# Three moves in the order of a hybrid pooling and attention block: products with the softmax reciprocals, sums of the h blocks, and one staging buffer

## The chip, the cores and the metric

The kernel runs on one core of one Trainium2 chip. The metric is the device time of one execution in microseconds (us). The kernel before takes 721.88 us, the median of three runs (721.56 to 722.66). Engines are named as the profile names them: PE (matmul), DVE (vector), ACT (scalar), POOL (GpSimd) and SP, whose queue issues most of the transfers.

## The reference

One decoder block on 1024 tokens, with 16 learned meta tokens ahead of them, all in float32:

```python
h = rmsnorm(concat(meta, x), norm_g)                                   # (1040, 1024)
u, z_pool, q, k, v, z_attn, f, g_pool, g_attn = split(h @ w_in)
y_pool = causal_multiscale_pool(u, pool_w, pool_scale) * silu(z_pool)  # windows 2, 4, 8, 16
y_attn = forgetting_attention(q, k, v, log_sigmoid(f + b_forget)) * silu(z_attn)   # 8 heads of 64
merged = sigmoid(g_pool) * (y_pool @ w_up_pool) + sigmoid(g_attn) * (y_attn @ w_up_attn)
out = rmsnorm(x + merged @ w_out, final_norm_g)
```

The attention is a causal softmax whose logits carry a running sum of the forget gates. The kernel leaves its rows unnormalised at first, sums the exponentials on the way, and multiplies the result y by the reciprocals of these sums later.

## The kernel before

Every float32 matrix is split into a high part and a remainder, and a product is made of three matmuls (high with high, high with remainder, remainder with high). The high part is copied by ACT, the remainder is a subtraction on POOL or DVE. Each weight tile thus goes through SP (load `raw`), ACT (`whi`), POOL (`wlo`), and then PE can use it.

The work has five stages, with their place in the profiled execution:

- **Projection steps (0 to 62 us, L495 to L574).** x is normalised, transposed on PE and split into `hh` and `hl` (L261). Between the transposes the first head pair is projected in twelve steps n = 0 to 11 (L526): q, k and v for four stretches of tokens. Each step of n > 3 also forms one half of a block of h, the sum or negated sum of `hh` and `hl` in a tile `f` of 128 x 1024 on DVE (`h_block`, L170), and stores it to DRAM (L177), where later sums build on it. SP's other transfers of these steps are small parameters (L553 to L555), the early weights of the next head pair (`load_raw`, L482), the pooling weights `pw` (L567) and copies from DRAM to DRAM that wait in a list and are issued one per step, and five more at the end (`copies`, L179, `gs` and `td`).
- **Attention (62 to 425 us).** 16 units of one head and 512 queries each. PE's gaps in them are filled from a list of projections (`Fill`, L415): first q of pair 1 (whose weights were loaded early), then u of group 3 (`f_u`, L403), then k of pair 1, and so on. `w_chunk` (L199) loads the weights of such a projection and splits them.
- **Chunks (425 to 551 us, L1147 to L1298).** z_pool, z_attn and half of g_attn are formed with seven block products n = 0 to 6 in place of eight, each in six chunks i of 12 matmuls with 512 columns (`g_prod`, L1059). A chunk is named (n, i). The loop at L1235 goes through them: it splits the weights of the chunk four places on (`w_split`, L1020), issues the matmuls of the chunk two places on, moves the result of the chunk before out of its PSUM bank (`evict`, L1104), and then does what the table `extra` (L1199) has for this chunk. Chunks with i > 3, and those of n = 1, 3 and 4, share four banks in rotation (`gb_`, L1054), so chunk (4, 5) writes the bank that (4, 1) wrote four chunks before and cannot start until `evict` has read that one.
- **Up projections (551 to 638 us)** and **output product and norm (638 us to the end).**

The table `extra` holds among others: `rc_in` (L926), which loads the reciprocals, one per head and query, from DRAM into `rc`; `attn_norm` (L932), one DVE multiplication of a 128 x 1024 tile y by `rc`; `pool_split` (L963), which splits a pooled group into `plh` (ACT) and `pll` (DVE); and `h_split` (L1037), which splits two halves of a block of h into `gh`, which the chunks of the next n multiply with. In n = 5 the order of i is 3, 2, 1, 0, 4, 5.

What sets the order: PE's order is that of the code everywhere (L88). In the projection steps and in the chunks the order of all engines is that of the code (L461 to L579, L1165 to L1300). Elsewhere a scheduler of the framework orders ACT, DVE, POOL and SP, and it may put an instruction of the attention stage among those of the projection steps. Each engine, and SP's queue, works strictly in its order: an instruction that waits holds up all behind it. SP's transfers use eight completion semaphores in turn, so SP issues a transfer only when the eighth before it has landed.

The pool `ap_` has six buffers with the tag "s" for the tiles of x, of `f`, for `pw` and later for the scores `S`; the pool `stg` has two with the tag "st" for results on their way to DRAM.

Of the kernel before, what the change touches and what calls it, by code (L numbers as in the profile page):

```python
# [8 lines left out]
F32 = mybir.dt.float32  # L9
# [44 lines left out]
def tile_hybrid_block(ctx, tc, x, meta, norm_g, w_in, b_forget, pool_w, pool_scale,  # L54
# [115 lines left out]
    def h_block(blk, k):  # L170
        f = ap_.tile([128, 2, 512], F32, name="f", tag="s", bufs=6)
        hi, lo = [hblock(d, blk)[:, k:k + 2] for d in (hh4, hl4)]
        if blk in ("12", "21"):
            nc.vector.scalar_tensor_tensor(f, hi, -1.0, lo, op0=ALU.mult, op1=ALU.subtract)
        else:
            nc.vector.tensor_tensor(f, hi, lo, op=ALU.add)
        nc.sync.dma_start(rows_of(HS[{"12": "C", "21": "X"}.get(blk, blk)])[:, k:k + 2], f)  # L177
# [345 lines left out]
    todo, early = [], {}  # L523
    for t0, t1 in ((0, 256), (256, 512), (512, 768), (768, L)):
        todo += [("q", t0, min(t1, SEQ)), ("k", t0, t1), ("v", t0, t1)]
    for n, (kind, t0, t1) in enumerate(todo):  # L526
        if n + 4 < 8:
            xts[n + 4] = norm_load(n + 4)
        if kind == "q":
            run(q_piece(0, wq, t0, t1))  # L530
        elif kind == "k":
            run(k_piece(0, wk, t0, t1))
        else:
            g = v_piece(0, wv, t0, t1)
            run(g)
        i = {0: 2, 1: 3, 3: 4, 4: 5, 5: 8, 6: 6, 7: 7}.get(n)
        if i is not None:
            norm_t(i, xts[i], ntok(i))
        if n == 0:
            hv_ = split_hi(rv, gp, "g")  # L540
            wv = split_lo(rv, hv_, gp, "g")
            VT[0] = gp.tile([128, L], F32, name="vt", tag="g")
            v_alloc(0)
        if n > 3:
            h_block(("11", "12", "22", "21")[n // 2 - 2], n % 2 * 2)
        i = {1: 4, 2: 5, 3: 8, 4: 6, 5: 7}.get(n)
        if i is not None:
            norm_scale(xts[i], ntok(i), norm_stat(xts[i], ntok(i)))
        if n == 2:
            zero_q(0)  # L550
        if n == 4:
            wf = at_.tile([128, KO, H], F32, name="wf", bufs=1)
            nc.sync.dma_start(wf, w_in2[:, :, COL_F:COL_F + H])  # L553
            nc.sync.dma_start(bfb, bass.AP(tensor=b_forget.tensor, offset=b_forget.offset, ap=[[0, 128], [1, H]]))
            nc.sync.dma_start(psc, pool_scale[0].rearrange("(g c) -> c g", c=128))  # L555
        if n == 8:
            wfs = at_.tile([128, KO, 2 * H], F32R, name="wfs", bufs=1)
            nc.vector.tensor_copy(wfs[:, :, :H], wf)
            nc.vector.tensor_tensor(wfs[:, :, H:], wf, r32(wfs[:, :, :H]), op=ALU.subtract)
        if n == 4:  # L560
            early["q"] = load_raw(COL_Q + 128)
        if n == 6:
            early["k"] = load_raw(COL_K + 128)
        if n > 3:
            copies(1)
        if n == 7:
            pw = ap_.tile([128, 4, 128], F32, name="pw", tag="s", bufs=6)  # L567
            nc.sync.dma_start(pw, pool_w[0].rearrange("g c d -> c g d"))
        if n == 10:
            nc.scalar.activation(pwh, pw, AF.Copy)  # L570
            nc.gpsimd.tensor_tensor(pwl, pw, r32(pwh), op=ALU.subtract)
        if n in (4, 7, 10):
            run(v_blocks(0, *range(max(1, 2 * (n // 3) - 2), 2 * (n // 3))))
# [358 lines left out]
    def attn_norm(p):  # L932
        nc.vector.tensor_tensor(Y[p], Y[p], RC[p], op=ALU.mult)
# [103 lines left out]
    def h_split(n):  # L1037
        op_h[n] = [[hq.tile([128, 2, 512], F32R, name="gh", tag="h") for _ in range(2)] for _ in range(2)]
        hi, lo = op_h[n]
        for k in range(2):  # L1040
            nc.scalar.activation(hi[k], raw_h[n][k], AF.Copy, scale=-1.0 if n == 2 else 1.0)
        for k in range(2):
            if n == 2:
                nc.vector.scalar_tensor_tensor(lo[k], raw_h[n][k], -1.0, r32(hi[k]), op0=ALU.mult, op1=ALU.subtract)
            else:
                nc.vector.tensor_tensor(lo[k], raw_h[n][k], r32(hi[k]), op=ALU.subtract)
# [30 lines left out]
    def silu(z, ps, scale=1.0):  # L1077
        evacs.append(nc.scalar.activation(z, ps, AF.Silu, scale=scale))  # L1078
# [112 lines left out]
    def steps_of(g):  # L1191
# [26 lines left out]
        (3, 4): [lambda: h_in(6)],  # L1218
        (3, 5): [lambda: pool_split(2)],
        
        (4, 1): [lambda: attn_norm(0), lambda: h_split(5)],
        (4, 2): [lambda: attn_norm(1), lambda: rc_in(2)],
        (4, 3): [lambda: pool_split(1)],
        (4, 4): [lambda: rc_in(3)],
        (5, 3): [lambda: h_split(6)],
        (5, 2): [lambda: attn_norm(2)],
        (5, 1): [lambda: attn_norm(3)],
        (5, 0): [lambda: pool_split(0), lambda: silu(za[0][:, T0_], za[0][:, T0_])],
        (5, 4): [lambda: silu(za[1][:, T0_], za[1][:, T0_]), lambda: silu(za[2][:, T0_], za[2][:, T0_])],
        (6, 4): [lambda: silu(za[3][:, T0_], za[3][:, T0_])],  # L1230
    }
    AH = 4
# [276 lines left out]
```

## Time and profile before

| what | value |
|---|---|
| median of three runs | 721.88 us |
| the profiled execution: its own time, its span | 722.76 us, 721.0 us |
| PE busy | 707.9 us, 98% of the span |
| DVE, ACT, POOL busy | 72%, 58%, 47% |
| DMA | 129.89 MB, mean 180 GB/s |

The span is the time from the first to the last instruction of the profiled execution; its own time has some 1.8 us more around it. In the rows of the timeline the columns are the start in us, the length in us, the engine, the line of the code, the operation with the tile it writes and those it reads, the shape, and how often it was repeated; in brackets stands how long the engine was idle before and what ended that. SPq rows are issues of transfers, not their landing. Rows of the waits name who waited, for whom, for how long in total, how often, and the longest.

### The profile page before, as it was taken

How to read it: one execution, taken by the hardware profiler on the slowest of the kernel's cores; microseconds unless marked ns; L12 is line 12 of the kernel's file. 1: busy time of each engine (PE TensorE's matmuls, PEld its weight loads, DVE VectorE, ACT ScalarE, POOL GpSimd, SP SyncE). 2: the span in 40 equal slices, each digit the busy share in tenths (PEclk: the TensorE clock that was granted, in tenths of full speed). 3: DMA queues.
4: the chain of work that ended last, by engine and by line, in shares of the span. 5: the costliest groups of instructions: out<-in, count | busy, mean ns of one | idle time of the engine just before them, and what ended most of it. 6: DMA issues, size and time to landing. Idle time of an engine off the chain costs nothing.

```text
span 721.0 us, 10896 instructions
## 1 busy us (share of the span) xinstructions
PE 707.9 (98%) x3613; PEld 610.3 (85%) x3613; DVE 517.5 (72%) x917; ACT 419.8 (58%) x928; POOL 340.6 (47%) x463
## 2 busy tenths in 40 slices
PE   8999999999999999999999999999899999999996
PEld 6997999998899888998888888888688888888885
DVE  5784488476888777787776937984867645888775
ACT  7654477676767779676666522445556332535445
POOL 5423247476275847566296832354882010007152
PEclk9999999999999999999999999999999999999998
DMA  9099987956534485556648459689808366761006
GB/s 315 21 303 359 334 255 173 216 121 161 118 106 100 126 210 128 142 112 132 171 144 214 110 182 348 187 214 284 254 31 273 117 220 236 267 229 59 0 1 233
DMA packets 95354, 129.89 MB, mean 180 GB/s; under 512 B 11457, under 2 KB 62657, under 8 KB 93266
## 3 DMA queue, kind: packets, MB, share of 16 engines
q1 hardware_dynamic: 91776, 110.32, 48.1%
q0 software_dynamic: 2224, 16.25, 12.2%
q10 hardware_dynamic: 1298, 2.63, 1.0%
q8 instruction: 28, 0.46, 0.2%
q14 instruction: 28, 0.23, 0.1%
HBM read 102.25 MB, written 58.39 MB: 223 GB/s over the span
## 4 chain that ended last, share of the span: by engine, by line
PE 93%; DVE 3%; ACT 2%; issue 1%; POOL 0%; POOLq 0%; ACTq 0%; DVEq 0%
PE pj L217 53%; PE pj L1070 12%; PE pj L1389 8%; PE po L794 5%; PE pt L1070 4%; PE pt L1389 2%; PE ps L730 2%; PE ps L729 2%; PE pj L590 1%; DVE pl L776 1%; PE pt L279 1%; PE pj L730 1%; PE pj L729 1%; ACT qa L315 1%; PE pn L279 0%
## 5 line engine op out<-in xcount | busy, mean ns | idle before, releaser
L217 PE MATMUL pj<-hh,whi 128*128 128x512 f32 (+3 forms) x576 | 127.1, 347 | 0.2 <-DVE ka L337 0.2
L217 PE MATMUL pj<-hh,wlo 128*128 128x512 f32 (+3 forms) x576 | 127.2, 346 | 0.0
L217 PE MATMUL pj<-hl,whi 128*128 128x512 f32 (+3 forms) x576 | 126.8, 345 | 0.0
L217 PEld LDWEIGHTS pj<-hh,whi 128*128 128x128 f32 x576 | 97.2, 188 | 10.7 <-PE pj L217 0.5
L217 PEld LDWEIGHTS pj<-hh,wlo 128*128 128x128 f32 x576 | 96.8, 188 | 10.0
L217 PEld LDWEIGHTS pj<-hl,whi 128*128 128x128 f32 x576 | 96.5, 188 | 9.7
L208 POOL TENSOR_TENSOR wlo<-raw,whi 128x256 fp32r<-128x256 f32 x100 | 74.8, 780 | 61.3 <-PE pj L217 31.7
L784 POOL TENSOR_TENSOR acc<-acc,S 128x256 f32<-128x256 f32 (+2 forms) x128 | 90.7, 728 | 8.3 <-ACT S L771 4.1
L776 DVE TENSOR_TENSOR pl<-S,ph 128x512 fp32r<-128x512 f32 (+4 forms) x112 | 80.0, 736 | 15.5 <-ACT ph L775 14.9
L1032 POOL TENSOR_TENSOR gw<-graw,gw 128x256 fp32r<-128x256 f32 x52 | 46.7, 928 | 52.8 <-ACT gw L1025 52.6
L1070 PE MATMUL pj<-gh,gw 128*128 128x512 f32 x276 | 66.2, 397 | 3.4 <-ACT zp L1078 3.4
L1070 PEld LDWEIGHTS pj<-gh,gw 128*128 128x128 f32 x276 | 52.6, 191 | 15.1 <-ACT zp L1078 3.8
L743 DVE TENSOR_TENSOR pt<-pt,S 128x400 f32<-128x400 f32 (+2 forms) x96 | 46.6, 485 | 20.7 <-ACT S L734 18.4
L771 ACT ACTIVATE S<-S 128x512 f32<-128x512 f32 (+4 forms) x112 | 50.3, 481 | 12.8 <-DVE S L770 12.5
L775 ACT ACTIVATE ph<-S 128x512 fp32r<-128x512 f32 (+4 forms) x112 | 52.7, 483 | 3.1 <-PE po L794 2.2
L770 DVE TENSOR_TENSOR S<-S,pt 128x512 f32<-128x512 f32 (+4 forms) x112 | 50.0, 499 | 0.6
L1025 ACT ACTIVATE gw<-graw 128x512 fp32r<-128x512 f32 x38 | 23.2, 623 | 36.6 <-DMA graw<-gs 18.9
L1282 DVE TENSOR_TENSOR rl<-pj,rl 128x512 f32<-128x512 f32 x32 | 22.0, 690 | 28.5 <-PE pj L217 27.8
L784 POOL TENSOR_TENSOR acc<-S 128x256 f32<-128x256 f32 (+1 forms) x32 | 29.6, 950 | 23.6 <-ACT S L771 20.5
L734 ACT ACTIVATE S<-ps,negc 128x16 f32<-128x16 f32 (+4 forms) x65 | 33.1, 514 | 10.4 <-PE ps L730 9.7
L794 PE MATMUL po<-ph,V 128*128 128x512 f32 (+4 forms) x112 | 36.4, 325 | 0.0
L1389 PE MATMUL pj<-opw 128*128 128x512 f32 (+1 forms) x168 | 36.2, 374 | 0.0
(249 smaller groups left out, 1392.7 us busy)
## 6 DMA issues: line engine op xcount, KB each, us to landing
raw<-in_w_in_dram SPq DMA_DIRECT2D x27, 512.0 KB, 6.4
gs<-in_w_in_dram SPq DMA_DIRECT2D x15, 512.0 KB, 9.9
gs<-gs POOLq DMA_DIRECT2D x4, 1536.0 KB, 13.2
graw<-gs SPq DMA_DIRECT2D x12, 512.0 KB, 7.9
td<-in_w_out_dram SPq DMA_DIRECT2D x10, 512.0 KB, 11.5
graw<-in_w_in_dram SPq DMA_DIRECT2D x9, 512.0 KB, 5.7
xt<-in_x_dram SPq DMA_DIRECT2D x8, 512.0 KB, 6.5
accd<-acc SPq DMA_DIRECT2D x16, 256.0 KB, 2.6
```

Of the source, the lines that this page charges most:

```text
L208: ins = nc.gpsimd.tensor_tensor(lo[:, k:k + 2], raw[:, k:k + 2], r32(hi[:, k:k + 2]), op=ALU.subtract)
L217: nc.tensor.matmul(ps, a, b, start=(i == 0), stop=(i == len(seq) - 1))
L743: nc.vector.tensor_tensor(m[:kb, c0:], m[:kb, c0:], s[:kb, c0:], op=ALU.max)
L770: nc.vector.tensor_tensor(s[:kb, c0:], s[:kb, c0:], self.pm[:kb, c0:], op=ALU.subtract)
L771: exps.append(nc.scalar.activation(s[:kb, c0:], s[:kb, c0:], AF.Exp))
L775: nc.scalar.activation(ph[:kb, c0:], s[:kb, c0:], AF.Copy)
L776: dves.append(nc.vector.tensor_tensor(pl[:kb, c0:], s[:kb, c0:], r32(ph[:kb, c0:]), op=ALU.subtract))
L784: accs.append(nc.gpsimd.tensor_tensor(acc[:kb, c:c1], (S0 if b == 1 else acc)[:kb, c:c1], s[:kb, c:c1], op=ALU.add))
L794: nc.tensor.matmul(self.po[:, c0:], v, self.P[b][i][:kb, c0:], start=(b == 0 and i == 0), stop=(b == self.nb - 1 and i == 1))
L1032: nc.gpsimd.tensor_tensor(op[:, 1, k:k + 2], raw[:, k:k + 2], r32(op[:, 0, k:k + 2]), op=ALU.subtract)
L1070: nc.tensor.matmul(ps, stat(n, i, p, k), op_h[n][q][k // 2][:, k % 2], start=fresh and m == 0, stop=m == 11, skip_group_check=True)
L1389: nc.tensor.matmul(ps, pick(A_, k, p)[:, i * 128:(i + 1) * 128], pick(B_, k, q)[:, c0:c1], start=start and n == 0, stop=n == 11, skip_grou ...
```

## The change

Three edits, and no computation is added or taken away. The eight halves of the h blocks are formed in steps 6 to 11 in place of one per step from 4 to 11: two each in steps 8 and 11. The tile `pw` comes from the pool `stg` in place of `ap_`. In the chunks `attn_norm(0)` moves from (4, 1) to (4, 3), `attn_norm(1)` from (4, 2) to (4, 4), `pool_split(1)` from (4, 3) to (4, 5) with `rc_in(3)` behind it, `attn_norm(3)` from (5, 1) to (5, 4) and `pool_split(0)` from (5, 0) to (5, 5).

```diff
--- before.py
+++ after.py
@@ -523,6 +523,8 @@
     todo, early = [], {}
     for t0, t1 in ((0, 256), (256, 512), (512, 768), (768, L)):
         todo += [("q", t0, min(t1, SEQ)), ("k", t0, t1), ("v", t0, t1)]
+    blocks = {6: [("11", 0)], 7: [("11", 2)], 8: [("12", 0), ("12", 2)], 9: [("22", 0)], 10: [("22", 2)],
+              11: [("21", 0), ("21", 2)]}
     for n, (kind, t0, t1) in enumerate(todo):
         if n + 4 < 8:
             xts[n + 4] = norm_load(n + 4)
@@ -541,8 +543,8 @@
             wv = split_lo(rv, hv_, gp, "g")
             VT[0] = gp.tile([128, L], F32, name="vt", tag="g")
             v_alloc(0)
-        if n > 3:
-            h_block(("11", "12", "22", "21")[n // 2 - 2], n % 2 * 2)
+        for blk, k in blocks.get(n, ()):
+            h_block(blk, k)
         i = {1: 4, 2: 5, 3: 8, 4: 6, 5: 7}.get(n)
         if i is not None:
             norm_scale(xts[i], ntok(i), norm_stat(xts[i], ntok(i)))
@@ -564,7 +566,7 @@
         if n > 3:
             copies(1)
         if n == 7:
-            pw = ap_.tile([128, 4, 128], F32, name="pw", tag="s", bufs=6)
+            pw = stg.tile([128, 4, 128], F32, name="pw", tag="st")
             nc.sync.dma_start(pw, pool_w[0].rearrange("g c d -> c g d"))
         if n == 10:
             nc.scalar.activation(pwh, pw, AF.Copy)
@@ -1218,15 +1220,17 @@
         (3, 4): [lambda: h_in(6)],
         (3, 5): [lambda: pool_split(2)],
         
-        (4, 1): [lambda: attn_norm(0), lambda: h_split(5)],
-        (4, 2): [lambda: attn_norm(1), lambda: rc_in(2)],
-        (4, 3): [lambda: pool_split(1)],
-        (4, 4): [lambda: rc_in(3)],
+        (4, 1): [lambda: h_split(5)],
+        (4, 2): [lambda: rc_in(2)],
+        (4, 3): [lambda: attn_norm(0)],
+        (4, 4): [lambda: attn_norm(1)],
+        (4, 5): [lambda: pool_split(1), lambda: rc_in(3)],
         (5, 3): [lambda: h_split(6)],
         (5, 2): [lambda: attn_norm(2)],
-        (5, 1): [lambda: attn_norm(3)],
-        (5, 0): [lambda: pool_split(0), lambda: silu(za[0][:, T0_], za[0][:, T0_])],
-        (5, 4): [lambda: silu(za[1][:, T0_], za[1][:, T0_]), lambda: silu(za[2][:, T0_], za[2][:, T0_])],
+        (5, 0): [lambda: silu(za[0][:, T0_], za[0][:, T0_])],
+        (5, 4): [lambda: attn_norm(3), lambda: silu(za[1][:, T0_], za[1][:, T0_]),
+                 lambda: silu(za[2][:, T0_], za[2][:, T0_])],
+        (5, 5): [lambda: pool_split(0)],
         (6, 4): [lambda: silu(za[3][:, T0_], za[3][:, T0_])],
     }
     AH = 4
```

In the order of instructions on the engines this shows as follows. First SP in the projection steps, from the last load of x (`xt_394`) on; `f` are the halves of the h blocks, `wf`, `bfb` and `psc` small parameters, the first `raw` the early weights of q of pair 1, `gs5` a copy from DRAM to DRAM. Before:

```order
L248 DMA xt_394<-in_x_dram 128x1024
L177 DMA hs11_137<-f_491 128x2x512
L553 DMA wf_501<-in_w_in_dram 128x8x8
L554 DMA bfb_122<-in_b_forget_dram 128x8
L555 DMA psc_121<-in_pool_scale_dram 128x4x1
L482 DMA raw_505<-in_w_in_dram 128x8x128
L181 DMA gs5_136<-in_w_in_dram 256x512
L177 DMA hs11_137<-f_553 128x2x512
```

And now:

```order
L248 DMA xt_394<-in_x_dram 128x1024
L555 DMA wf_498<-in_w_in_dram 128x8x8
L556 DMA bfb_122<-in_b_forget_dram 128x8
L557 DMA psc_121<-in_pool_scale_dram 128x4x1
L482 DMA raw_502<-in_w_in_dram 128x8x128
L181 DMA gs5_136<-in_w_in_dram 256x512 x2
L177 DMA hs11_137<-f_603 128x2x512
```

Six transfers that stood behind the first or the second store of an h block now stand ahead of the first.

Second, SP at the end of these steps. `raw_1013` holds the weights of u of group 3, the second projection that PE takes in the attention stage. Before, the scheduler had it right behind `pw`:

```order
L181 DMA gs1_132<-in_w_in_dram 256x512
L568 DMA pw_662<-in_pool_w_dram 128x4x128
L202 DMA raw_1013<-in_w_in_dram 128x8x128
L177 DMA hs22_138<-f_697 128x2x512
L181 DMA gs1_132<-in_w_in_dram 256x512
```

Now it stands behind the last two of the copies, `td5` and `td1`, that end these steps:

```order
L177 DMA hsX_142<-f_812 128x2x512
L181 DMA gs3_134<-in_w_in_dram 256x512
L181 DMA gs3_134<-in_w_in_dram 512x256
L181 DMA td5_131<-in_w_out_dram 256x512 x2
L181 DMA td1_127<-in_w_out_dram 256x512 x2
L202 DMA raw_1013<-in_w_in_dram 128x8x128
L181 DMA gs2_133<-in_w_in_dram 256x512 x2
```

The load of `raw_1013` moved from the 28th place of SP's transfers to the 41st; the transfers up to the 41st place are the same set in both. On ACT and POOL the split of these weights (`whi_1019`, `wlo_1020`) moved later with it; on PE nothing changed its place.

Third, DVE in the chunks of n = 4, from the eviction of (4, 0) on (`zp_5217`); `zp_5219`, `zp_5221` and `zp_5223` are the evictions of (4, 1), (4, 2) and (4, 3), `gh` the split of the block of h for n = 5, `y` with `rc` is `attn_norm`. Before:

```order
L1081 TENSOR_TENSOR zp_5217<-pj_5212,zp_5217 128x512
L933 TENSOR_TENSOR y_5441<-y_5441,rc_5775 128x1024
L1046 TENSOR_TENSOR gh_5865<-hraw_5643,gh_5863 128x1024
L1046 TENSOR_TENSOR gh_5866<-hraw_5644,gh_5864 128x1024
L1029 TENSOR_TENSOR gw_5871<-graw_5708,gw_5871 128x512
L1081 TENSOR_TENSOR zp_5219<-pj_5213,zp_5219 128x512
L933 TENSOR_TENSOR y_5535<-y_5535,rc_5778 128x1024
L1081 TENSOR_TENSOR zp_5221<-pj_5214,zp_5221 128x512
L967 TENSOR_TENSOR pll_5915<-u_5292,plh_5914 128x1024
L1081 TENSOR_TENSOR zp_5223<-pt_5215,zp_5223 128x512
```

And now:

```order
L1083 TENSOR_TENSOR zp_5217<-pj_5212,zp_5217 128x512
L1048 TENSOR_TENSOR gh_5864<-hraw_5643,gh_5862 128x1024
L1048 TENSOR_TENSOR gh_5865<-hraw_5644,gh_5863 128x1024
L1031 TENSOR_TENSOR gw_5870<-graw_5708,gw_5870 128x512
L1083 TENSOR_TENSOR zp_5219<-pj_5213,zp_5219 128x512
L1083 TENSOR_TENSOR zp_5221<-pj_5214,zp_5221 128x512
L935 TENSOR_TENSOR y_5441<-y_5441,rc_5775 128x1024
L1083 TENSOR_TENSOR zp_5223<-pt_5215,zp_5223 128x512
L935 TENSOR_TENSOR y_5535<-y_5535,rc_5778 128x1024
```

The first multiplication with the reciprocals stands behind the split of the h block, one weight split and the evictions of (4, 1) and (4, 2), all of which stood behind it before.

## The prediction

> **What bounds the kernel now.** I read the page first: the span, the busy times, then the row of PE in 40 slices.
>
> ```profile
> span 721.0 us, 10896 instructions
> PE 707.9 (98%) x3613; PEld 610.3 (85%) x3613; DVE 517.5 (72%) x917; ACT 419.8 (58%) x928; POOL 340.6 (47%) x463
> PE   8999999999999999999999999999899999999996
> ```
>
> PE is busy for 98%. Only 13.1 us are left in which a change of order can bring matmuls closer together, and any wait that it makes on PE is added to the time in full. So I asked next for PE's waits, which name almost all that is not start and end:
>
> ```profile
> PE pj L1070 <- ACT zp L1078: 3.4, 1, 3.4
> PE pt L279 <- DVE hl L282: 0.8, 1, 0.8
> PE pt L279 <- DVE hl L271: 0.2, 1, 0.2
> ```
>
> One wait of 3.4 us lies in the chunks, two small ones in the projection steps. These are the places that the change touches. The timeline of the chunks shows where the long one comes from (rows of several engines in order of time):
>
> ```profile
> 495.60 0.68 DVE L1081 TENSOR_TENSOR zp<-pj,zp 128x512 f32<-128x512 f32 x1
> 498.42 2.00 ACT L1041 ACTIVATE gh<-hraw 128x1024 fp32r<-128x1024 f32 x2
> 498.45 2.37 SPq L930 DMA_DIRECT2D rc<-recs  x4
> 501.77 2.88 PE L1070 MATMUL pj<-gh,gw 128*128 128x512 f32 x12
> 503.18 1.23 DVE L933 TENSOR_TENSOR y<-y,rc 128x1024 f32<-128x1024 f32 x1 [6.89 <-DMA rc<-recs]
> 504.32 2.35 DVE L1046 TENSOR_TENSOR gh<-hraw,gh 128x1024 fp32r<-128x1024 f32 x2
> 506.60 0.68 DVE L1029 TENSOR_TENSOR gw<-graw,gw 128x512 fp32r<-128x512 f32 x1
> 507.20 0.69 DVE L1081 TENSOR_TENSOR zp<-pj,zp 128x512 f32<-128x512 f32 x1
> 508.03 4.57 PE L1070 MATMUL pj<-gh,gw 128*128 128x512 f32 x12 [3.38 <-ACT zp L1078]
> ```
>
> DVE stands 6.89 us at the first `attn_norm`, whose reciprocals are on their way from DRAM. Behind it on DVE stand the split of the h block, a weight split and the eviction of (4, 1), which ends at 507.89. PE starts (4, 5) at 508.03: that chunk writes the bank of (4, 1). The row of the waits names an ACT instruction that ended just then (507.96), but it is the eviction that PE needed. The wait costs more than its length, as the windows show (us, PE busy with its instructions, the clock granted, DMA share, GB/s):
>
> ```profile
> 500.00:504.40 4.40, 4.40 (x21) 1.00 1.00 236
> 504.60:508.00 3.40, 0.05 (x1) 1.00 1.02 364
> 509.00:512.30 3.30, 3.30 (x9) 0.50 1.08 263
> ```
>
> After the pause the clock is at half for 3.3 us, so (4, 5) takes 4.57 us.
>
> **The change part by part: the chunks.** A chunk takes 2.72 us (2.88 less the overlap of 0.16 with the next). Without the wait (4, 5) would follow at 501.77 + 2.72 = 504.5 and its successor at 507.2. That one began at 508.03 + 4.57 less 0.16, 512.4. At stake are 5.2 us: 3.5 of pause and 1.7 of half clock.
>
> In the new order DVE goes from `zp` (to 496.3) to the split of the h block as soon as ACT has its halves (about 499.5 and 500.4), to 501.9; the weight split to 502.5; the eviction of (4, 1) to 503.2, 1.3 us before PE wants the bank. The eviction of (4, 2) ends at 503.8, and only then comes the first `attn_norm`, 0.6 us after the time at which it ran before (503.18). The second follows at about 505.5. What is late next? The pooling split now stands at (4, 5), its ACT half behind two Silu instructions and its DVE half ending about 509.7. The weights of (5, 2), (5, 1) and (5, 4) are finished on POOL, in turn with sums that wait for the evictions:
>
> ```profile
> 500.39 1.44 POOL L136 TENSOR_TENSOR zp<-zp 128x256 f32<-128x256 f32 x2
> 507.96 3.38 POOL L136 TENSOR_TENSOR zp<-zp 128x256 f32<-128x256 f32 x2 [6.13 <-DMA hraw<-hs]
> 515.04 1.90 POOL L1032 TENSOR_TENSOR gw<-graw,gw 128x256 fp32r<-128x256 f32 x2
> ```
>
> From the eviction at 503.2 on, with the slow price of the sum (3.38, once it took 1.44): sum to 506.6, weights of (5, 2) to 508.5, sum to 511.9, weights of (5, 1) to 513.8. PE would start (5, 1) at 512.6 and reach the remainder after eight matmuls, at 514.4. So 0.6 us are left at the least. `rc_in(3)` comes behind the split whose tile it overwrites, at about 510 to 513, lands by 520, and `attn_norm(3)` asks for it at about 519; behind that stand only a weight split and evictions that PE needs after 523. `pool_split(0)` feeds the last of the four pooling products. I cost these moves at nothing; a failing cover costs one to three us. Chunks: **-5.2 us**, between -5.3 and -3.
>
> **The projection steps.** DVE and PE around the first two halves of the h blocks:
>
> ```profile
> 33.43 1.22 DVE L176 TENSOR_TENSOR f<-hh,hl 128x1024 f32<-128x1024 f32 x1
> 36.79 1.22 DVE L176 TENSOR_TENSOR f<-hh,hl 128x1024 f32<-128x1024 f32 x1
> 37.02 0.63 PE L279 MATMUL pt<-ident,xt 128*128 128x128 f32 x4 [0.15 <-DVE hl L271]
> 38.77 0.75 DVE L258 SCALAR_TENSOR_TENSOR xt<-xt,rstd,gb 128x512 f32<-128x512 f32 x1 [0.77 <-POOL rstd L126]
> 40.98 1.29 DVE L282 TENSOR_TENSOR hl<-pt,hh 128x512 fp32r<-128x512 f32 x2
> 41.73 0.65 PE L279 MATMUL pt<-ident,xt 128*128 128x128 f32 x4 [0.77 <-DVE hl L282]
> ```
>
> Without the first `f` all of DVE up to the last scaling of x comes 1.1 us earlier, and both waits of PE go, with some 0.2 us of starting up behind them: PE is 0.15 + 0.77 + 0.2 = **1.1 us** ahead from 42 us on. The moved halves lie where DVE waited anyway; the doubled ones of step 11 end near 57, before DVE is needed for the gates.
>
> The stores and loads matter more. These are SP's issues around the place, and the landings of single transfers, the last number of the rows from the DMA view (of the first store at 34.67, the raw load at 51.34 and the copy at 63.43):
>
> ```profile
> 15.81 0.33 SPq L248 DMA_DIRECT2D xt<-in_x_dram  x1
> 34.67 0.38 SPq L177 DMA_DIRECT2D hs<-f  x1
> 51.34 0.37 SPq L202 DMA_DIRECT2D raw<-in_w_in_dram  x1
> 63.43 1.63 SPq L181 DMA_DIRECT2D td<-in_w_out_dram  x1
> ```
>
> ```profile
> hs<-f SPq DMA_DIRECT2D x1, 512.0 KB, 2.9
> raw<-in_w_in_dram SPq DMA_DIRECT2D x1, 512.0 KB, 5.7
> td<-in_w_out_dram SPq DMA_DIRECT2D x1, 512.0 KB, 14.9
> ```
>
> ```profile
> 20.00:34.00 14.00, 14.00 (x123) 13.84 (x122) 10.56 (x18) 10.32 (x25) 6.38 (x13) 1.00 0.01 2
> 42.00:80.00 38.00, 38.00 (x246) 32.59 (x245) 21.43 (x48) 16.22 (x37) 12.28 (x15) 1.00 1.05 352
> ```
>
> From 42 to 80 us the DMA engines are saturated (share 1.05), and what is queued lands ever later after its issue. Before, the weights of u of group 3 were loaded at 51.34 and landed at 57.0. Their split and use:
>
> ```profile
> 57.05 1.15 ACT L206 ACTIVATE whi<-raw 128x512 fp32r<-128x512 f32 x2 [0.57 <-DMA raw<-in_w_in_dram]
> 57.76 3.40 POOL L208 TENSOR_TENSOR wlo<-raw,whi 128x256 fp32r<-128x256 f32 x4 [0.38 <-ACT whi L206]
> 74.23 1.57 PE L217 MATMUL pj<-hh,whi 128*128 128x384 f32 x8
> ```
>
> So they lay ready 16 us before PE came to them at 74.23. Now this load is the last of the same set of transfers, issued at about 64, and the queue decides when it lands. The last of this set, the copy issued at 63.43, landed at 63.43 + 14.9 = 78.3. What differs is the start. SP's queue was blocked from 16.2 to 34.67 by the store of the first `f`; now six transfers ahead of that store (three of 512 KB) run from 16 us, when the DMA engines did nothing (share 0.01). But SP then waits, with an empty queue, for the new first `f`, which ends at about 42.4 (the row at 40.98: less 1.1, plus 1.29 and 1.22). At 42.4 some 22.5 transfers were left before, worked off by 78.3: 1.6 us each. Now 21.5 are left, one less, since two copies are done and one store of `f` is added and the rest of a copy was under way. But the first transfer alone needs 2.9 us and not 1.6. So the landing is estimated at 78.3 - 1.6 + 1.3 = 78.0, with 76 to 79.5 as its bounds. The first half of `whi` (0.6 us) is ready at 78.7, 4.5 us later than PE's start before. PE asks at 74.2 - 1.1 = 73.1, so it pauses 5.6 us, and the 1.1 us are lost inside this wait. The pause is longer than that of the chunks, so half clock follows, 3.3 us of it or **1.7 us**. `wlo` (2.8 to 3.4 us from the first half on) is asked for 2.8 us after the start and then at half clock: nothing. Queued behind the late weights are on ACT the weights of k of pair 1 and the eviction of q, on SP the next raw load, which overwrites this tile: none is needed by PE before 84 us. Projection steps: **+6.2 us**, from +4.2 to +7.7.
>
> The sum is 6.2 - 5.2 = +1.0 us against the profiled execution, 722.76 to 723.8. That execution lies 0.9 us above the median of the runs shown; taken over to the median 721.88 it is **722.9 us**.
>
> The Trainium skill has two rules here. "TensorE: Matmul & The Clock Gate" (Part 1, the HAM clock gate) lets the clock fall to half after a whole idle window of about 3.4 us, and the windows run freely. A pause of 5.6 us holds a whole window only if it falls well, and by this rule the 1.7 us may be missing. The trace agrees with the halving but saw it after a pause of 3.4 us, 0.05 us of it busy. "DMA: Bandwidth & Descriptors" (Latency and other measured facts) puts the fixed cost of a transfer at about 2 us, and its table of bandwidth gives 6.15 us for 1 MB; by these a 512 KB load issued at 64 would land at about 69, estimated, and PE would not wait. The row of 14.9 us speaks against that in this stretch.
>
> **The rivals.** First, the late load is hidden anyway: it lands by 72.4, as an issue at 64 with the 5.7 us of the raw row would. Then PE keeps the 1.1 us and the chunks their 5.2: 721.9 - 6.3 = 715.6 us. For it: the row of 5.7 us. Against it: seven transfers are under way ahead of the load, at 1.6 us each, and a landing at 76 would still leave half the pause. Chance 0.14.
>
> Second, slower: POOL becomes late in n = 5. Its place is the remainder of the weights of (5, 1), 0.6 us ahead of PE by the slow prices; from there on each us that POOL loses is one of PE, up to some 2.5 us, which is below the length that halved the clock. With the forecast's +1.0 that gives 722.9 + 2.5 = 725.4 us. For it: DVE and ACT are at work beside it all the time, and one row of the sums shows more than twice the price of the other. Against it: with the price of the other, 1.44, some 4 us are left. Chance 0.11.
>
> Third, the pause at 73 us is not followed by half clock, or is cut by its window: 722.9 - 1.7 = 721.2 us. For it: the place of the window is not known. Against it: the windows around 508. Chance 0.09.
>
> **How the numbers follow.** My forecast has 0.66: both mechanisms as priced. Its own range is 720.9 to 724.6, from a landing of the load at 76 to 79.5. About 0.2%, or 1.4 us, is what a measurement of this kernel can tell from no change: 720.4 to 723.3. Of the 0.66 some 0.35 lie within it, 0.28 above and 0.03 below. The first rival gives 0.14 faster, the second 0.11 slower, the third 0.07 same and 0.02 faster. Together: faster 0.19, same 0.42, slower 0.39. The range for 8 in 10 reaches down to a load that lands nearly in time, 717.0, and up to the second rival, 725.5.
>
> **What would show it.** In the profile of the changed kernel: SP's load of these weights issued near 64 us and landing after 76; ACT idle before `whi` for it; a wait of PE of 4 to 6 us before the first 384-column matmuls; half clock right behind that; no wait of PE at L279 near 41; DVE's wait for `rc` under 1 us and no wait of PE in the chunks. I am wrong if PE takes up u of group 3 without a pause, if it still waits in the chunks, or if a new wait appears at the last chunks of n = 5.

## The result, and the profile after

The changed kernel takes 727.15 us, the median of six runs (726.34 to 728.93), beside 722.07 us for the kernel before on the same chip (720.42 to 723.05): a ratio of 1.0074, with a 95% interval of 1.0057 to 1.0092. It is slower by some 5 us, where about 1 us was forecast; the time lies above the range. The profiled execution has a span of 725.7 us, 4.7 more than before.

The page of the changed kernel, the same three rows as before:

```profile
span 725.7 us, 10898 instructions
PE 708.7 (98%) x3613; PEld 611.7 (84%) x3613; DVE 522.6 (72%) x917; ACT 419.5 (58%) x928; POOL 343.0 (47%) x463
PE   8999699999999999999999999999999999999995
```

A 6 stands in the fifth slice, at 73 to 91 us, where a 9 stood. The waits of PE (who waits, for whom, us in total, how often, the longest) name the place:

```profile
PE pj L217 <- ACT whi L206: 6.1, 1, 6.1
...
PE pj L217 <- DVE zp L908: 0.8, 1, 0.8
PE pj L1072 <- DVE gx L1083: 0.5, 1, 0.5
```

The wait of 3.4 us in the chunks and those for `hl` in the projection steps are gone. In their place stand one of 6.1 us for `whi` and two new ones that the prediction did not have. The first, in the timeline (start, length, engine, line, what; in brackets the idle time and what ended it), with the landing of the load as the last number of the DMA view's row:

```profile
64.99 0.73 SPq L202 DMA_DIRECT2D raw<-in_w_in_dram  x1
68.46 2.41 ACT L315 ACTIVATE qa<-pj 64x512 fp32r<-64x512 f32 x4 [1.01 <-PE pj L217]
79.28 2.19 ACT L206 ACTIVATE whi<-raw 128x512 fp32r<-128x512 f32 x4 [8.41 <-DMA raw<-in_w_in_dram]
71.89 1.97 PE L217 MATMUL pj<-hh,wlo 128*128 128x512 f32 x8
79.96 2.93 PE L217 MATMUL pj<-hh,whi 128*128 128x384 f32 x8 [6.10 <-ACT whi L206]
```

```profile
raw<-in_w_in_dram SPq DMA_DIRECT2D x1, 512.0 KB, 14.3
```

The load is issued at 64.99 and lands 14.3 us later, at 79.3. ACT stands 8.41 us at `whi`; PE takes up u of group 3 at 79.96 in place of 74.23. The windows behind it (us, PE busy and its instructions, then the other engines, the clock granted, DMA share, GB/s):

```profile
73.86:79.96 6.10, 0.01 (x1) 0.00 (x0) 0.00 (x0) 0.68 (x2) 0.00 (x0) 0.79 1.04 356
79.96:84.27 4.31, 4.31 (x13) 4.31 (x14) 0.34 (x1) 3.87 (x7) 4.23 (x7) 0.50 0.61 193
84.27:88.00 3.73, 3.73 (x23) 3.73 (x23) 1.03 (x2) 0.49 (x1) 1.34 (x2) 1.00 1.19 352
```

PE works at half clock for 4.3 us. In the chunks the mechanism of the prediction shows as it was written:

```profile
507.11 3.00 DVE L1048 TENSOR_TENSOR gh<-hraw,gh 128x1024 fp32r<-128x1024 f32 x2 [3.19 <-ACT gh L1043]
509.98 5.60 PE L1072 MATMUL pj<-gh,gw 128*128 128x512 f32 x24
511.17 1.27 DVE L1083 TENSOR_TENSOR zp<-pj,zp 128x512 f32<-128x512 f32 x2
512.37 1.38 DVE L935 TENSOR_TENSOR y<-y,rc 128x1024 f32<-128x1024 f32 x1
```

The evictions of (4, 1) and (4, 2) come ahead of the first multiplication with the reciprocals, and PE runs from (4, 4) into (4, 5) without a pause and at full clock. Then, at the second of the four pooling products:

```profile
536.91 0.33 SPq L1101 DMA_DIRECT2D sp_ga<-ge  x1
537.33 0.39 SPq L1261 DMA_DIRECT2D rawu<-in_w_up_pool_dram  x1
540.10 0.63 ACT L1264 ACTIVATE whu<-rawu 128x512 fp32r<-128x512 f32 x1 [4.44 <-DMA rawu<-in_w_up_pool_dram]
540.77 0.85 DVE L1265 TENSOR_TENSOR wlu<-rawu,whu 128x512 fp32r<-128x512 f32 x1 [3.98 <-ACT whu L1264]
541.54 1.40 DVE L908 SCALAR_TENSOR_TENSOR zp<-pj,psc,zp 128x512 f32<-128x512 f32 x2
542.33 0.50 PE L217 MATMUL pj<-plh,pwh 128*128 128x512 f32 x1 [0.85 <-DVE zp L908]
```

The first weights of the up projection (`rawu`) are loaded behind a store on SP, and SP stands 11.5 us at that store, until POOL has formed the sum that it stores. DVE stands 3.98 us at their split, and behind that stands the scaling that frees a pooling bank (`zp`, L908), for which PE waits.

Taken matmul by matmul, the start of one and the same matmul after less before, the way to the 4.7 us is: +5.7 us at the start of u of group 3 and +2.05 of half clock behind it, which makes +7.8 at 84.3 us; of this some 0.3 are made up little by little in the attention stage, so that +7.45 are left at its end; +0.7 at a chunk of n = 3, the wait for `gx`; -5.2 at (4, 5); +1.0 at the second pooling product (538.36 to 542.33 is +3.97). The last matmuls stand at +4.1. The remaining 0.6 us lie behind them: from the end of PE's last matmul to the end of the span there are 7.41 us here and 6.76 before. This stretch goes with the pool of `pw`: over the traces of all runs below it is 7.41 to 7.45 us in seven of the eight with `pw` in `stg` (e10 has 6.76), and 6.54 to 6.99 in the nine with `pw` in `ap_`. What connects the two stays open.

### The profile page after: what moved, and what is told of

Its sections match the earlier page's. It is cut to its first block, busy times and chain, and to the rows that moved or that the text cites. A ratio compares the mean times of both kernels' runs of the same rounds, so it can differ in the third digit from the quotient of the medians.

```text
span 725.7 us, 10898 instructions
## 1 busy us (share of the span) xinstructions
PE 708.7 (98%) x3613; PEld 611.7 (84%) x3613; DVE 522.6 (72%) x917; ACT 419.5 (58%) x928; POOL 343.0 (47%) x463
## 4 chain that ended last, share of the span: by engine, by line
PE 83%; DMA 8%; DVE 4%; issue 2%; ACT 1%; SPq 0%; POOL 0%; POOLq 0%; ACTq 0%; DVEq 0%
PE pj L217 52%; PE pj L1393 8%; PE pj L1072 6%; PE po L796 5%; PE pt L1393 2%; DMA raw<-in_w_in_dram 2%; PE pt L1072 2%; PE ps L732 2%; DMA graw<-gs 2%; PE ps L731 2%; DMA zp<-accd 1%; DMA hsX<-f 1%; DMA pw<-in_pool_w_dram 1%; PE pj L732 1%; DVE zp L983 1%
## 5 line engine op out<-in xcount | busy, mean ns | idle before, releaser
L217 PE MATMUL pj<-hh,whi 128*128 128x512 f32 (+3 forms) x576 | 128.8, 351 | 6.4 <-ACT whi L206 6.1
L217 PEld LDWEIGHTS pj<-hh,whi 128*128 128x128 f32 x576 | 98.8, 192 | 17.2 <-ACT whi L206 6.5
L1034 POOL TENSOR_TENSOR gw<-graw,gw 128x256 fp32r<-128x256 f32 x52 | 48.6, 960 | 52.9 <-ACT gw L1027 52.8
L1072 PE MATMUL pj<-gh,gw 128*128 128x512 f32 x276 | 64.3, 390 | 0.5 <-DVE gx L1083 0.5
L206 ACT ACTIVATE whi<-raw 128x512 fp32r<-128x512 f32 x50 | 29.5, 626 | 12.3 <-DMA raw<-in_w_in_dram 8.4
```

What stands on the lines that cost most here:

```text
L217: nc.tensor.matmul(ps, a, b, start=(i == 0), stop=(i == len(seq) - 1))
L1034: nc.gpsimd.tensor_tensor(op[:, 1, k:k + 2], raw[:, k:k + 2], r32(op[:, 0, k:k + 2]), op=ALU.subtract)
L1072: nc.tensor.matmul(ps, stat(n, i, p, k), op_h[n][q][k // 2][:, k % 2], start=fresh and m == 0, stop=m == 11, skip_group_check=True)
```

## The experiments

The theory has three parts: the late load of `raw_1013` costs the 7.45 us; the moves in the chunks gain 5.2; and something that they move gives back 1 to 2. The rivals were that the new order of the h blocks costs by itself, that the chunks' moves are worth nothing in the end, and, for the late load, that it is late for another reason than its place. Medians stand beside those of the kernel before on the same chip; "ratio" is to that kernel, with its 95% interval.

**e1: only the moves in the chunks.** Against the change:

```diff
-    blocks = {6: [("11", 0)], 7: [("11", 2)], 8: [("12", 0), ("12", 2)], 9: [("22", 0)], 10: [("22", 2)],
-              11: [("21", 0), ("21", 2)]}
+    blocks = {n: [(("11", "12", "22", "21")[n // 2 - 2], n % 2 * 2)]
+              for n in range(4, 12)}
...
-            pw = stg.tile([128, 4, 128], F32, name="pw", tag="st")
+            pw = ap_.tile([128, 4, 128], F32, name="pw", tag="s", bufs=6)
```

> Only the moves in the chunks; the blocks of h and pw as before. Theory (the chunk moves take away the 5.2 us at (4,5), and pool_split(0) at (5,5) gives back 1.1 us at the pooling products; the +0.7 us that the change shows in a chunk of n = 3, where nothing was moved, comes with its late start of the attention stage or by chance): 722.1 - 5.2 + 1.1 = 718.0 us, 717.3 to 718.9; no wait at (4,5), a wait of PE of about 0.8 us at the second half of the second pooling product. Rival (the moves in the chunks are worth nothing in the end, since n = 5 takes back what n = 4 gives): 721 us or more.

718.55 us beside 722.45, ratio 0.996 (0.9941 to 0.9979), as the theory had it. The gain is real, and it is not all that (4, 5) gave: PE waits 0.88 us at the second pooling product (ahead of its first half, not its second) and 0.5 us in n = 3 here too. Two rows of the trace, SP and DVE:

```profile
529.98 0.39 SPq L1261 DMA_DIRECT2D rawu<-in_w_up_pool_dram  x1
533.55 0.71 DVE L1265 TENSOR_TENSOR wlu<-rawu,whu 128x512 fp32r<-128x512 f32 x1 [4.11 <-ACT whu L1264]
```

So the wait in n = 3 does not need the changes in the projection steps.

**e2: only the pool of `pw`.** Against the kernel before:

```diff
-            pw = ap_.tile([128, 4, 128], F32, name="pw", tag="s", bufs=6)
+            pw = stg.tile([128, 4, 128], F32, name="pw", tag="st")
```

> Only pw in the pool stg; the blocks of h and the chunks as before. In the order of SP the load raw_1013 stands behind the td copies here too. Theory (the late load is what costs, and the pool of pw alone is what moved it): PE waits 4 to 7 us for whi before u of group 3, half clock follows, 722.1 + 6 to 8 = 728 to 730 us. Rival (the new order of the blocks of h costs the time, by its stores that are issued late and together): within 1 us of the kernel before.

733.89 us beside 722.45, ratio 1.0169 (1.0142 to 1.0195). The one line alone moves the load behind the copies; why the scheduler answers a change of this pool in that way, no run shows. It costs more than the whole change, and 4 us more than the upper end of what was expected. ACT, DVE and PE show why it costs so much:

```profile
78.26 1.15 ACT L206 ACTIVATE whi<-raw 128x512 fp32r<-128x512 f32 x2 [9.68 <-DMA raw<-in_w_in_dram]
79.32 2.38 ACT L315 ACTIVATE qa<-pj 64x512 fp32r<-64x512 f32 x4
81.73 1.39 DVE L319 SCALAR_TENSOR_TENSOR ql<-pj,qa 64x512 fp32r<-64x512 f32 x2 [10.67 <-ACT qa L315]
83.27 0.98 PE L217 MATMUL pj<-hh,whi 128*128 128x384 f32 x2 [8.27 <-DVE ql L319]
```

The load lands at 78.2, a us earlier than in the change. But the scheduler put `whi` ahead of the four copies `qa` on ACT here, while in the change it stands behind them. So the eviction of q of pair 1 waits for the load too, and PE waits for the bank that it empties, until 83.27.

**e3: only the new order of the h blocks.** Against the kernel before, with the table `blocks` of the change:

```diff
-        if n > 3:
-            h_block(("11", "12", "22", "21")[n // 2 - 2], n % 2 * 2)
+        for blk, k in blocks.get(n, ()):
+            h_block(blk, k)
```

> Only the new order of the blocks of h; pw in ap_ and the chunks as before. In the order of SP raw_1013 stands at the 20th place of the list, ahead of five stores of blocks, here. Theory (the late load is what costs): no wait before u of group 3, and the two small waits of the transposes near 40 us go: 722.1 - 0.5 to 1.1 = 721.0 to 721.6 us. Rival (the new order of the blocks costs the time): 727 us or more.

722.93 us beside 722.45, ratio 1.0013 (0.9995 to 1.0031): neither the small gain of the theory nor the loss of the rival. No wait for u of group 3, and PE is 0.7 us ahead there. It is given back in the scores: the next load, k of pair 1, lands at 88.4 in place of 85.2 (the first store of an h block is issued at 42.4 in place of 34.7; I take this for the reason, no run tells it apart). ACT waits for it with the scores behind:

```profile
88.46 1.15 ACT L206 ACTIVATE whi<-raw 128x512 fp32r<-128x512 f32 x2 [3.27 <-DMA raw<-in_w_in_dram]
96.48 0.50 PE L731 MATMUL ps<-qa,ka 128*128 128x512 f32 x1 [0.44 <-ACT S L736]
```

**e4: the change, with the load five transfers further ahead.**

```diff
-    copies(5)
+    copies(0)
```

> The whole change, but the five copies that end the projection steps are left in the list, so that raw_1013 stands five transfers further ahead and the copies come behind it; the same copies are made later. Theory (the saturated queue decides when the load lands, some 1.6 us for each transfer ahead of it): landing near 79.3 - 5 x 1.6 = 71.3 us, whi ready at 72, PE asks at 73.8 and does not wait: 727.1 - 8 = 719 us (718.5 to 719.7). Rival (the load lands late for another reason, such as the completion semaphores or its own 512 KB in a busy queue): a wait of 3 us or more stays, 723 us or more.

722.70 us beside 722.45, ratio 1.0016 (0.9995 to 1.0037). The first half of the theory held better than written: issued at 59.07, the load landed at 69.4. The second failed. PE still waited, 3.1 us. That is the sign which the rival had named, but the load was not late; what PE waited for was `ql`:

```profile
69.47 1.15 ACT L206 ACTIVATE whi<-raw 128x512 fp32r<-128x512 f32 x2 [6.90 <-DMA raw<-in_w_in_dram]
...
72.25 2.39 ACT L315 ACTIVATE qa<-pj 64x512 fp32r<-64x512 f32 x4
```

```profile
75.26 1.38 DVE L319 SCALAR_TENSOR_TENSOR ql<-pj,qa 64x512 fp32r<-64x512 f32 x2
...
76.79 1.49 PE L217 MATMUL pj<-hh,whi 128*128 128x384 f32 x4 [3.10 <-DVE ql L319]
```

Here the scheduler put `whi` ahead of the Exp and Ln of the gates and of `qa` on ACT. The load lands 4 us before PE asks, at 73.7, and so is in time for PE, but it is too late for an ACT that stands at `whi` from 62.6 us on with all of this queued behind.

**e5: e4 with `whi` behind the four `qa` copies on ACT**, and **e6: e2 with the same edge.**

```diff
-            nc.scalar.activation(hi[:, k:k + 4], raw[:, k:k + 4], AF.Copy)
+            cps = nc.scalar.activation(hi[:, k:k + 4], raw[:, k:k + 4], AF.Copy); col != COL_U + 384 or after(cps, qhis[-5])
...
-            nc.scalar.activation(QA[p, e][r, c0:c1], ps[rows(e)[0]], AF.Copy, scale=0.125)
+            qhis.append(nc.scalar.activation(QA[p, e][r, c0:c1], ps[rows(e)[0]], AF.Copy, scale=0.125))
```

The list `qhis` collects the `qa` copies, and `whi` of u of group 3 is ordered behind the last one of the first half of q.

> As e4 (the whole change, with the five copies behind the load), and whi of u of group 3 is ordered on ACT behind the four qa copies of the first half of q of pair 1. In e4 the load landed at 69.4 us, yet PE waited 3.1 us, for ql: ACT stood 6.9 us at whi with the Exp and Ln of the gates and the qa copies queued behind it. Theory (ACT's place for whi is the second half of the cost): ACT does Exp, Ln and the qa copies first, ql ends near 72, whi is ready by 72, PE asks at 73.6 and does not wait, no half clock: 722.7 - 4.2 = 718.5 us. Rival (the copies themselves, moved behind the load, slow something else): 721 us or more.

> As e2 (only pw in stg), and whi ordered on ACT behind the same four qa copies. The load is as late as in e2. Theory: PE now waits for the load alone and not for ql behind it: whi half ready at 78.9 in place of ql at 83.1, so PE starts u of group 3 some 4.2 us earlier than in e2, with half clock still behind the pause: 733.9 - 4.2 = 729.7 us. Rival (the place on ACT does not matter, the late load is all): 733 us or more.

e5: 719.31 us beside 722.22, ratio 0.9964 (0.9944 to 0.9985), 0.8 us above the expectation; e6: 728.33 beside 722.22, ratio 1.008 (1.0048 to 1.0112), 5.6 us less than e2, a little more than expected. PE in e5 goes into u of group 3 at 73.58 without a pause (it waits 1.1 us later, at the second pooling product); in e6 it starts at 78.64 in place of 83.27 and waits for the load alone:

```profile
70.65 1.14 ACT L206 ACTIVATE whi<-raw 128x512 fp32r<-128x512 f32 x2
...
73.58 1.57 PE L217 MATMUL pj<-hh,whi 128*128 128x384 f32 x8
```

```profile
78.64 1.83 PE L217 MATMUL pj<-hh,whi 128*128 128x384 f32 x8 [3.59 <-ACT whi L206]
```

So the late load has two prices: what PE waits for its own weights, and what stands behind the waiting `whi` on ACT. In the change, where `qa` stands ahead of `whi` on ACT (68.46 and 79.28), only the first is paid.

**e7: e1 with `pool_split(0)` at (6, 5)**, and **e8: the change with `pw` in `ap_` and `pool_split(0)` at (6, 5).**

```diff
-        (5, 5): [lambda: pool_split(0)],
...
+        (6, 5): [lambda: pool_split(0)],
```

> As e1 (only the moves in the chunks), with pool_split(0) at (6,5) in place of (5,5), where DVE and ACT stood idle for 4 us. Theory (pool_split(0) at (5,5) stands ahead of the eviction of (5,5), and sum, store, load, split and pooling bank follow that one): the wait of 0.9 us at the second half of the second pooling product goes, 718.6 - 1.0 = 717.5 us. Rival (that wait comes from attn_norm(3) at (5,4) or from the shorter path of PE): no change, 718.6 us, or the last pooling product then waits for its late half.

> The change with two things taken back or mended: pw in ap_ as before (so raw_1013 keeps its early place on SP), and pool_split(0) at (6,5). Theory (the late load costs 7.5 us, pool_split(0) 1 us, and the new order of the blocks gains 0.6 us that it gives back in the first scores, where e3 showed the weights of k of pair 1 landing 3 us later): as e7, 717.5 us, within 1 us of it. Rival (the blocks' new order is a gain once the load is early): 716.5 us or less.

e7: 718.65 us beside 722.22, ratio 0.9947 (0.9925 to 0.9968); e8: 718.55 beside 722.22, ratio 0.9942 (0.9918 to 0.9966). In e7 the theory fell and the rival's figure came: with the split out of the way the wait of PE stayed, at 1.22 us. DVE and PE:

```profile
528.22 1.37 DVE L969 TENSOR_TENSOR pll<-u,plh 128x1024 fp32r<-128x1024 f32 x1
532.92 1.30 DVE L1265 TENSOR_TENSOR wlu<-rawu,whu 128x512 fp32r<-128x512 f32 x1 [3.33 <-ACT whu L1264]
...
534.94 0.50 PE L217 MATMUL pj<-plh,pwh 128*128 128x512 f32 x1 [1.22 <-DVE zp L908]
```

What DVE waits for is still `whu`, that is, the load: it stands idle for 3.33 us ahead of that split, so neither `pool_split(0)` nor `attn_norm(3)` ahead of it holds it up. In e8 the wait of PE is absent (the new order of the blocks as such brings no gain: 718.55 where the rival had 716.5 or less), and in e4 too, with the split at (5, 5). What goes with the size of the wait is how POOL stands to PE before (4, 5). Its weight splits near 493 us, against the trace before and with PE's own shift taken off, were early by 0.1, 0.3, 0.4, 0.5, 0.6, 1.0 and 2.1 us in e12, e7, e5, the change, e1, e8 and e4; PE then lost 1.9, 1.4, 1.3, 1.0, 1.0, 0.0 and 0.0 us at the second pooling product. These are seven traces that run together, not a cause shown: no run moves POOL alone.

**e9, e10, e11: the first up weights, load and split, later**, behind the first two pooling products in place of ahead of the first; on e1, on e5, and on the change with `pw` in `ap_`.

```diff
-    ws[0, 0] = up_weights(0, 0)
...
+        if n == 1: ws[0, 0] = up_weights(0, 0)
```

> As e1 (only the moves in the chunks, pool_split(0) at (5,5)), and the first load of up weights with its split is issued one pooling product later, so that on DVE the first four scalings of pooling products stand ahead of that split. Theory (DVE waits some 4 us at the split for this load, behind a store that waits for a sum on POOL; the scalings that free the pooling banks stand behind it): the wait of 1.0 us at the second half of the second pooling product goes, 718.6 - 1.0 = 717.6 us; no wait of PE for a scaling in the trace. Rival (PE is ahead of DVE by itself there, since the pause at (4,5) is gone): the wait stays, 718.6 us.

> As e5 (the whole change with the five copies behind the load of raw_1013 and whi behind the qa copies), and the first up weights one pooling product later as in e9. Theory: e5's wait of 1.1 us for a scaling goes, 719.3 - 1.2 = 718.1 us. Rival: the wait stays, 719.3 us.

> The change with pw in ap_ as before, pool_split(0) at (5,5) as in the change, and the first up weights one pooling product later. Theory: none of the three waits (u of group 3, chunk (4,5), second pooling product) is left, about as e8, 717.5 to 718.5 us. Rival (pool_split(0) at (5,5) costs by itself): 719 us or more.

All beside 722.50: e9 723.56, ratio 1.0012 (0.9999 to 1.0026); e10 722.87, ratio 1.0006 (0.9994 to 1.0018); e11 724.91, ratio 1.0033 (1.0018 to 1.0049). The wait at the second pooling product goes in all three, and a longer one, of 3.3 to 4.0 us, comes at the last, the fourth, where the split now stands ahead of a scaling. DVE and PE in e9:

```profile
545.29 0.69 DVE L1265 TENSOR_TENSOR wlu<-rawu,whu 128x512 fp32r<-128x512 f32 x1 [6.78 <-ACT whu L1264]
...
546.70 0.79 PE L217 MATMUL pj<-plh,pwh 128*128 128x512 f32 x1 [3.96 <-DVE zp L908]
```

All three expectations were missed, but the runs name the wait: it follows the split of these weights wherever that stands.

**e12: the change once more.**

> The change itself once more, for a second trace. Theory: what the order fixes comes again (the load of raw_1013 landing near 79 us, a wait of 6 us, some 2 us of half clock, no wait at (4,5)); the wait of 0.5 us in n = 3 and that at the second pooling product depend on how late POOL and DVE are against PE when the chunks begin, and may be gone. About 727 us.

727.35 us beside 722.50, ratio 1.0056 (1.0038 to 1.0075). The load lands at 78.7, PE waits 5.7 us for `whi`, half clock behind it, no wait at (4, 5). The wait in n = 3 is absent, that at the second pooling product is 1.7 us.

**e13, e14, e15: only the load of the first up weights earlier**, at (5, 2), ahead of two stores of SP; its split stays. On e1, on e5, and on the change with `pw` in `ap_`.

```diff
-        (5, 2): [lambda: attn_norm(2)],
+        (5, 2): [lambda: attn_norm(2), lambda: raw0.append(up_raw(0, 0))],
...
-        raw = wp.tile([128, 4, 128], F32, name="rawu", tag="raw")
-        nc.sync.dma_start(raw, (wup_p, wup_a)[a][:, :, j * 128:(j + 1) * 128])
+        raw = raw0.pop() if raw0 else up_raw(j, a)
```

> As e1 (only the moves in the chunks), with only the load of the first up weights moved on SP from behind the store of the sum to ahead of two stores, some 8 us earlier; its split stays where it was on ACT and DVE. Theory (DVE stands some 4 us at the split for this load, and the scaling that frees the pooling bank stands behind it): DVE's wait for whu goes, so does PE's wait of 1.0 us for the scaling, and no longer one comes in its place: 718.6 - 1.0 = 717.6 us. Rival (DVE is late by itself): the wait stays, 718.6 us.

> As e5 (the whole change with the five copies behind the load of raw_1013 and whi behind the qa copies), with the load of the first up weights early as in e13. Theory: e5's wait of 1.1 us for a scaling goes, 719.3 - 1.2 = 718.1 us. Rival: the wait stays, 719.3 us.

> The change with pw in ap_ as before and the load of the first up weights early as in e13. Theory: none of the three waits is left, as e8 or a little better, 717.5 to 718.5 us. Rival (pool_split(0) at (5,5) costs by itself): 719 us or more.

Here `up_raw` holds the two lines taken out of `up_weights`. All beside 723.88: e13 718.60, ratio 0.9939 (0.9914 to 0.9964); e14 717.84, ratio 0.9926 (0.9902 to 0.995); e15 718.47, ratio 0.9937 (0.9915 to 0.9959). In none of the three traces does PE wait at a pooling product, as the theory had it. SP and DVE in e13:

```profile
522.09 0.38 SPq L1202 DMA_DIRECT2D rawu<-in_w_up_pool_dram  x1
...
529.25 0.72 DVE L1271 TENSOR_TENSOR wlu<-rawu,whu 128x512 fp32r<-128x512 f32 x1
530.15 1.45 DVE L908 SCALAR_TENSOR_TENSOR zp<-pj,psc,zp 128x512 f32<-128x512 f32 x2 [0.17 <-PE pj L217]
```

DVE no longer waits for the load but for PE. The traces show this; the times alone do not: e13's 718.60 is the rival's figure, and its interval overlaps that of e1. The whole mended change (e14) has the lowest median of the runs and is faster than both kernels; the intervals of e1, e5, e7, e8, e13, e14 and e15 overlap, so their order among each other is not settled. e15, with `pool_split(0)` at (5, 5), is no slower than e8 with it at (6, 5), so its rival, that this place costs by itself, finds no support.

## Why the prediction was wrong, point by point

- **What bounds the kernel, and which places:** right. PE's waits decided, and the two places named were the two large terms.
- **The wait and the half clock at (4, 5):** right in mechanism and size for this execution: -5.2 us, the eviction of (4, 1) ahead of the first `attn_norm`, full clock. It was the price of one execution, though. Where the chunks are as before, the same wait is 3.4 us in the trace before, 3.0 in e2, 2.3 in e6 and 1.9 in e3, and half clock follows it only in the first and in e6 (the last section shows why).
- **"I cost these moves at nothing; a failing cover costs one to three us":** this is one step that failed. 1.7 us came back: 1.0 at the second pooling product and 0.7 in n = 3. The prediction looked for what is late next among the weights of n = 5, and the second rival put it on POOL at (5, 1). What was late stood further on: the first up weights, loaded behind a store that waits for a sum, and the scalings behind their split on DVE. That DVE waits for this load is nothing new (2.98 us in the trace before); what is new is that PE is there in time to feel it. e13 to e15 show that with the load early the wait is gone. That the stop at (4, 5) had hidden it is a reading of the traces: where the pause and half clock are both there (before, e6) PE loses nothing at that place, where only the pause is (e2, e3) it loses 0.45 and 0.27 us, and without either 0 to 1.9. The 0.7 us in n = 3, where the prediction had no term at all, appear in four traces (the change, e1, e10 and e11) and not in e12, the same kernel as the change; the cause stays open, as does why POOL stands to PE as it does when (4, 5) comes.
- **The late load:** this is the other step that failed: right in mechanism, too small in size, +7.45 us where +6.2 was written. The half clock cost 2.05 us where 1.7 was written, since PE met 4.3 us of it and not 3.3; some 0.3 were made up later. The start came 5.7 us later and not 4.5, because the load landed at 79.3 and not at 78.0. The rate was right: from the first landing, 45.69, to 79.26 there are 21 more at 1.60 each. The count of what was left was half a transfer short, and the first landed 3.2 us after its issue in place of 2.9. The cause is not the h blocks (e3) but the pool of `pw` (e2); the prediction showed the moved load and did not say which edit moved it.
- **"The 1.1 us are lost inside this wait":** right. PE was 1.0 us ahead at 42; at 51 DVE, at work on the doubled halves of an h block, held it up, and 0.55 were left at 73. It changed nothing in the sum, as written, but without the late load it is given back again in the attention stage (e3).
- **"Queued behind the late weights are on ACT ...: none is needed by PE before 84 us":** right for the order of this kernel, which the scheduler chose. Ahead of the four `qa` copies, the same `whi` makes PE start 4.6 us later (e2 against e6).
- **The range and the chances:** the sum of +1.0 had each term's error on the same side: +1.25 for the load, +1.7 for the covers, +0.6 at the end, for which there was no term. Both terms came out inside the bounds written beside them, +7.45 in +4.2 to +7.7 and -3.5 (the 5.2 less the 1.7) in -5.3 to -3; but the forecast's own range was taken from the load's bounds alone (722.9 + 1.5 is 724.4, too, and not 724.6). With the upper bounds of both, 7.7 - 3 = +4.7, it would have reached 726.6, short of the measured time by about the 0.6 of the end. The range of 717.0 to 725.5 allowed one failing cover or a late load at its bound, not both. The third rival and the first fell with the first wait. By the Trainium skill's "DMA: Bandwidth & Descriptors" (Latency and other measured facts, and its table of bandwidth, which was measured with transfers issued from GpSimd) the load would have landed near 69, estimated, some 5 us after its issue. The trace agrees for 512 KB on an empty queue (3.2 and 4.8 us for those issued at 42.47 and 42.95), not for what is queued behind others: 14.3 us here, 10.4 even in e4.

## What to carry to other kernels

A removed pause also removes the time in which the other engines caught up: after costing the gain, follow every engine's next waits for loads past the place of the change, above all a load that stands on its queue behind a store that waits. Where a scheduler orders the engines, look up what a change of a pool or a buffer moves, and for each late load look at two things: when it lands, and what stands behind the instruction that waits for it. A wait read from one execution has a spread of its own, and so has the half clock behind it; a gain is not more certain than they are. And where two terms have bounds, the range of the sum needs both.

## What the runs showed of the hardware that was not expected

How long PE pauses does not alone decide whether half clock follows. The wait of 2.27 us at (4, 5) in e6 was followed by 3.4 us of it, that of 3.04 us in e2 was not. The PE clock is the number behind the five busy times; first e6, with the stretch of the pause ahead of it, then e2:

```profile
510.30:513.46 3.16, 0.89 (x5) 0.53 (x4) 3.16 (x5) 3.00 (x5) 0.66 (x1) 1.00 1.06 372
513.46:516.88 3.42, 3.42 (x10) 2.66 (x9) 3.42 (x6) 0.66 (x2) 3.42 (x3) 0.50 1.10 282
```

```profile
518.10:521.50 3.40, 3.35 (x15) 2.83 (x16) 3.40 (x5) 0.51 (x1) 3.40 (x3) 1.00 1.11 324
```

In e3 1.86 us went without it. The waits of 3.1 us (e4), 3.3 (e10) and 3.6 (e6, at u of group 3) were followed by one stretch of 3.4 us, those of 3.7 (e11), 4.0 (e9), 5.7 (e12), 6.1 (after) and 8.3 us (e2) by one of 6.8, twice as long.

What decides is where the pause falls. In each of the 17 traces all changes of the granted clock lie whole multiples of 3.413 us apart (in the kernel before: up at 10.59, down at 508.94, up at 512.35). If PE's idle time is counted in windows of this grid, from the first rise of the clock on, one rule fits all traces: full clock turned to half behind each of the 27 windows in which PE was idle for 1.94 us or more, and behind none in which it was idle for 1.73 us or less. The pause of e6 lies whole in one window, from 510.05 to 513.46, with 2.27 us. That of e2 is cut by a window's end at 516.80 into 1.69 and 1.35 us, that of e3 into 0.71 and 1.15. The pause of 3.38 us in the kernel before was cut as well, into 0.88 and 2.50. So the 1.7 us of half clock in the -5.2 hung on the place of the window, while a pause of 5.6 us, wherever it lies, leaves at least 2.8 us in one window. The Trainium skill, "TensorE: Matmul & The Clock Gate" (Part 1, the HAM clock gate), has windows of about 3.4 us that run freely and asks for one whole idle window. The lengths and the grid agree with such windows; the halvings behind windows with 1.94 (e9) to 3.1 us (e4) of idle time do not agree with a whole idle one.
